# Measured durations in the planner of a two-block network kernel, and small-column 1/sqrt on ScalarE with a Newton step on VectorE instead of GpSimd's pow

## The chip, the cores and the metric

One core of one Trainium2 chip runs the whole program. The metric is the device time of one execution in microseconds. The five instruction streams of the core are called here PE (TensorE), ACT (ScalarE), DVE (VectorE), POOL (GpSimd) and SP (SyncE, which here only issues transfers).

## The reference

Two blocks run one after the other on one sequence of 512 rows of 1024 numbers in float32; each has two layers. Cut to the parts that the text speaks of:

```python
def _rmsnorm(x, g):
    y = xf * lax.rsqrt(jnp.mean(xf * xf, axis=-1, keepdims=True) + EPS)
    return (y * g.astype(jnp.float32)).astype(x.dtype)
...
for l in range(DEPTH):                      # first block, DEPTH = 2
    z = _rmsnorm(x, g_pre_mix[l]) @ w_in[l]
    y_f = _fourier_mix(zf, w_fourier[l])
    y_a = _window_attn(rope(zq), rope(zk), v, sink[l])
    mkv = _rmsnorm(mem, g_mem[l]) @ w_mem_kv[l]
    y_m = _memory_attn(zm, km, vm)
    y = concat([_rmsnorm(y_f), _rmsnorm(y_a), _rmsnorm(y_m)]) @ w_out[l]
    x = x + _rmsnorm(y, g_post_mix[l])
    h = _rmsnorm(x, g_pre_ffn[l])
    x = x + _rmsnorm((silu(gate) * up) @ w_ffn_out[l], g_post_ffn[l])
...
for l in range(DEPTH):                      # second block
    x = x + 0.5 * swiglu(rms_norm(x, ffn1_norm[l]), ffn1_w1[l], ffn1_w2[l])
    x = x + hybrid_mixer(rms_norm(x, mix_norm[l]), ...)   # RG-LRU, MLA attention, conformer convolution, gates
    x = x + 0.5 * swiglu(rms_norm(x, ffn2_norm[l]), ffn2_w1[l], ffn2_w2[l])
return rms_norm(x, final_norm)
```

## The kernel before

Activations lie transposed, as tiles of 128 features by 512 rows (slots named `s`, 100 of them); every product is made of three passes of TensorE over a high and a low half in a reduced type (h by l, l by h, h by h), so that one 128x128 block of a weight costs three matmuls of 512 columns. Weights come in three steps: POOL issues a transfer of the high half, ACT or DVE scales it by -1 into the low half's slot, and POOL issues a second transfer that adds the weight onto it. Sums build up in 8 PSUM banks (`ps`).

Nothing is issued in the order of the code. The code records every operation in a `Plan`; `price` (L391) gives each a length in us, and `schedule` (L423) is a list scheduler that plays the five engines against these lengths: an operation's due time comes from the running sum of TensorE's lengths ahead of its consumers, free slots and PSUM banks are counted, a transfer lands after a modelled time, and of the operations that are ready the one due first is taken. A `copy` or `scale` may go to ACT or DVE, whichever would be done first. The order that comes out is issued at L646, so all instructions of the trace stand on that one line, and groups have to be told apart by their tiles.

The root mean square of a norm is made in two ways. `inv` (L800) sums the squares with four or two one-column matmuls (`ps<-ones,s` with `128x1`), DVE makes `rms` (mean plus EPS, 128 partitions by 4 or 2 columns), POOL raises it to the power -1/2 in one instruction (`rinv<-rms,nhalf`), DVE multiplies an identity by it and a matmul (`ps<-s,ones`) spreads it over the partitions; there are 19 of these. `wide` (L819) makes the sum on all partitions with two matmuls (`ps<-s,onesr`) and then the root on ACT, the reciprocal and four more steps on DVE, all 512 columns wide. ACT's functions live in tables; a change from exp or silu to the root shows in the trace as `ACT_TABLE_LOAD`.

Of the kernel before, what the change touches and what calls it, by code (L numbers as in the profile page):

```python
# [15 lines left out]
AF = mybir.ActivationFunctionType  # L16
ALU = mybir.AluOpType
# [298 lines left out]
class Plan:  # L316
# [76 lines left out]
    def price(self, way, outs, ins):  # L393
        eng, fn, _, kw = way
        width = lambda v: int(np.prod(v.shape[1:]))
        n = width(outs[0]) if eng == "tensor" else max([width(v) for v in outs + ins if v.shape[0] > 1] or [1])
        psum = any(v.tile.psum for v in outs + ins)
        cols = sum(isinstance(kw.get(k), View) for k in ("scalar1", "scalar2", "scalar", "bias", "scale"))
        if eng == "sync":
            return 128 * n * 4 / 330e3  # L400
        if eng == "tensor":
            if fn == "transpose":
                return 0.11
            if ins[0].tile.dtype == F32:
                return 2 * max(0.107, 0.427 * n / 512)
            return max(0.107, 0.213 * n / 512 + 0.003)
        if eng == "scalar":
            return 0.093 + n * 0.833e-3 + 0.093 * (cols > 0) + (0.1 if "accum_out" in kw else 0.0)
        if eng == "vector":
            if fn == "reciprocal":  # L410
                return 0.07 + 6.25e-3 * n
            if fn in ("tensor_scalar", "tensor_copy", "memset") and not psum:
                return 0.07 + 0.52e-3 * n + 0.06 * (cols > 0)
            return 0.07 + 1.04e-3 * n + (0.06 if fn == "scalar_tensor_tensor" else 0.0)
        if fn == "dma_start":
            return 0.6
        if kw.get("op") == ALU.pow:
            return 0.95
        if fn == "tensor_scalar":
            return 0.25 + (3.36e-3 if cols else 0.65e-3) * n  # L420
        return 0.07 + 2.25e-3 * n

    def schedule(self):  # L423
# [28 lines left out]
        state = {"table": None, "dma": 0.0}  # L452
        now = 0.0
# [91 lines left out]
        while done < len(self.ops):  # L545
            moved = True
            while moved:
                moved = False
                for e in self.ENGINES:
                    while idle_at[e] <= now + 1e-9 and queues[e]:  # L550
                        op = choose(e, pe[front].need if front < len(pe) else 1e9)
# [17 lines left out]
                        if e == "sync":  # L569
                            state["dma"] = max(state["dma"], now + 0.5) + cost  # L570
                            op.end, idle_at[e] = state["dma"] + 1.6, now + 0.06
                        elif op.fn == "dma_start":
                            n = int(np.prod(op.kw["out"].shape[1:]))
                            passes = 2 if "accum_op" in op.kw else 1
                            state["dma"] = max(state["dma"], now + 1.0) + passes * 128 * n * 4 / 330e3
                            op.end = state["dma"] + 1.6
                        heapq.heappush(events, (op.end, op.index, op))
                        for t in op.tiles:
                            t.ends[e] = max(t.ends.get(e, 0.0), op.end)
# [26 lines left out]
            now = events[0][0]  # L606
            while events and events[0][0] <= now + 1e-9:
                op = heapq.heappop(events)[2]
# [54 lines left out]
class Net:  # L663
# [141 lines left out]
    def inv(self, parts, d, n=4):  # L805
        nc = self.nc
        pv = self.ps()
        for i, p in enumerate(parts):
            for j in range(n):
                nc.tensor.matmul(pv[:, j:j + 1], p[:, 128 * j:128 * j + 128], self.ones[:, 0:1],  # L810
                                 start=i == 0 and j == 0, stop=i == len(parts) - 1, skip_group_check=True)
        v = self.small(n, name="rms")
        nc.vector.tensor_scalar(out=v, in0=pv[:, 0:n], scalar1=1.0 / d, scalar2=EPS,
                                op0=ALU.mult, op1=ALU.add)
        r = self.small(n, name="rinv")
        nc.gpsimd.tensor_tensor(out=r, in0=v, in1=self.nhalf[:, 0:n], op=ALU.pow)
        return r

    def wide(self, parts, d):  # L819


        nc = self.nc
        ps = self.ps()
        for i, p in enumerate(parts):
            h, l = self.split_t(p)
            nc.tensor.matmul(ps, self.onesr, l, start=i == 0, stop=False)
            nc.tensor.matmul(ps, self.onesr, h, start=False, stop=i == len(parts) - 1)
        v = self.t()
        nc.vector.tensor_scalar(out=v, in0=ps, scalar1=1.0 / d, scalar2=EPS, op0=ALU.mult, op1=ALU.add)
        r = self.t()  # L830
        nc.scalar.activation(out=r, in_=v, func=AF.Sqrt)
        nc.vector.reciprocal(out=r, in_=r)
        self.tt(v, r, out=v)
        self.tt(v, r, out=v)
        nc.vector.tensor_scalar(out=v, in0=v, scalar1=-0.5, scalar2=1.5, op0=ALU.mult, op1=ALU.add)
        return self.tt(r, v, out=r)
# [912 lines left out]
```

## Time and profile before

| what | value |
|---|---|
| runs of the kernel before | 3479.14, 3483.54, 3483.74 us, median 3483.54 |
| the profiled execution's own time | 3481.36 us |
| its span (first to last instruction) | 3479.6 us |
| PE busy | 3404.2 us (98%), 16296 matmuls |
| DVE, ACT, POOL busy | 1923.0, 893.1, 1748.9 us |
| granted TensorE clock, mean of the span | 0.992 |

The span is one execution seen by the hardware profiler; busy time of an engine is the sum over its instructions. PE is the engine to look at, so what matters of the other engines is where PE waited for them. 1.9 us of the profiled execution's time lie outside the span.

### The profile page before, as it was taken

The page shows a single profiled execution, that of the slowest core. Times are in us where ns is not written, and L with a number is a line of the kernel's source. Part 1 is how long each engine was busy: PE and PEld are TensorE (multiplying, and loading weights), DVE is VectorE, ACT ScalarE, POOL GpSimd, SP SyncE. Part 2 cuts the span into 40 slices and gives each one's busy share as a digit, 9 for nine tenths or more (in the row PEclk, how much of TensorE's full clock was granted, in tenths as well). Part 3 has the DMA queues.
Part 4 walks back from the last instruction along what each step waited for, and adds up shares of the span by engine and source line. Part 5 has one row for each costly group of instructions (what it writes and reads, how often), then busy time and mean ns, then how long its engine had stood idle before and what let it go on. Part 6 is the DMA issues. An engine that isn't in the chain of part 4 may idle for free.

```text
span 3479.6 us, 44666 instructions
## 1 busy us (share of the span) xinstructions
PE 3404.2 (98%) x16296; PEld 2844.1 (82%) x16296; DVE 1923.0 (55%) x3916; ACT 893.1 (26%) x1732; POOL 1748.9 (50%) x2433
## 2 busy tenths in 40 slices
PE   6999999899999999999999999999999999999998
PEld 4788888778888988888888888888888888888887
DVE  7964433876432733259997534244423999744332
ACT  5741002543000301016723200010001573411000
POOL 2455464364446544653456544664465336654462
PEclk8999999999999999999999999999999999999999
DMA  6688897798789887985899977998799669998794
GB/s 174 145 186 184 164 207 148 156 193 183 153 169 208 207 181 157 239 212 103 172 197 249 220 152 158 220 204 200 150 225 219 130 130 222 230 239 160 158 202 104
DMA packets 360444, 635.93 MB, mean 183 GB/s; under 512 B 40608, under 2 KB 63904, under 8 KB 360224
## 3 DMA queue, kind: packets, MB, share of 16 engines
q0 software_dynamic: 346752, 612.56, 82.4%
q1 hardware_dynamic: 13472, 20.52, 1.9%
q8 instruction: 128, 2.10, 0.2%
q14 instruction: 92, 0.75, 0.1%
HBM read 624.00 MB, written 6.29 MB: 181 GB/s over the span
## 4 chain that ended last, share of the span: by engine, by line
PE 90%; DVE 4%; DMA 2%; issue 1%; ACT 1%; POOL 1%; SPq 0%; POOLq 0%; DVEq 0%; ACTq 0%
PE ps L646 90%; DVE s L646 4%; ACT s L646 1%; DMA s<-in_x 1%; POOL s L646 0%; DMA s<-in_b_in 0%; DMA s<-in_pos 0%; DMA s<-in_a_in 0%; DMA s<-s 0%; POOL rinv L646 0%; DVE mx L646 0%; DMA s<-in_a_out 0%; DMA s<-in_a_mk 0%; SPq L646 0%; DVE sp L646 0%
## 5 line engine op out<-in xcount | busy, mean ns | idle before, releaser
L646 PE MATMUL ps<-s 128*128 128x512 f32 (+2 forms) x15706 | 3350.9, 376 | 44.6 <-DVE s L646 32.4
L646 PEld LDWEIGHTS ps<-s 128*128 128x128 f32 (+1 forms) x15706 | 2775.6, 188 | 587.9 <-DVE s L646 29.7
L646 POOL DMA_DIRECT2D s<-in_b x1088 | 786.0, 1024 | 666.2 <-DVE s L646 312.2
L646 ACT ACTIVATE s<-s 128x512 fp32r<-128x512 f32 (+2 forms) x702 | 396.9, 601 | 1713.0 <-DVE s L646 1142.4
L646 DVE TENSOR_TENSOR s<-ps,s 128x512 f32<-128x512 f32 (+4 forms) x642 | 397.9, 637 | 580.8 <-PE ps L646 571.6
L646 DVE TENSOR_SCALAR s<-s 128x512 fp32r<-128x512 f32 (+2 forms) x847 | 341.5, 422 | 486.3 <-DMA s<-in_b 283.9
L646 POOL DMA_DIRECT2D s<-in_a_f x544 | 397.4, 1089 | 354.3 <-DVE s L646 199.3
L646 DVE TENSOR_TENSOR s<-s 128x512 f32<-128x512 f32 (+2 forms) x822 | 500.7, 626 | 64.1 <-ACT s L646 36.5
L646 POOL DMA_DIRECT2D s<-in_b_in x368 | 290.4, 1030 | 263.4 <-ACT s L646 84.0
L646 DVE SCALAR_TENSOR_TENSOR s<-s,vecs 128x256 fp32r<-128x256 f32 (+25 forms) x446 | 288.3, 680 | 6.3 <-ACT s L646 3.2
L646 ACT ACTIVATE s<-s,vecs 128x512 f32<-128x512 f32 (+2 forms) x221 | 139.5, 652 | 307.1 <-DVE s L646 294.2
L646 DVE SCALAR_TENSOR_TENSOR s<-ps,s 128x512 f32<-128x512 f32 (+1 forms) x33 | 22.3, 674 | 187.2 <-PE ps L646 187.0
L646 ACT ACT_TABLE_LOAD x68 | 87.2, 1283 | 42.0 <-DVE s L646 40.2
L646 ACT ACTIVATE s<-ps 128x512 f32<-128x512 f32 (+1 forms) x40 | 21.4, 534 | 274.0 <-PE ps L646 251.9
L646 DVE CAST s<-s 128x512 fp32r<-128x512 f32 x192 | 83.8, 436 | 6.5 <-DMA s<-in_pos 1.1
L646 POOL DMA_DIRECT2D s<-in_a_in x64 | 47.2, 931 | 76.2 <-DVE s L646 24.4
L646 DVE RECIPROCAL s<-s 128x128 f32<-128x128 f32 (+1 forms) x46 | 76.5, 1673 | 7.8 <-ACT s L646 7.8
L646 ACT ACTIVATE s<-s,nb 128x256 f32<-128x256 f32 (+3 forms) x128 | 70.6, 553 | 25.9 <-DVE nb L646 25.7
L646 POOL DMA_DIRECT2D s<-in_a_out x64 | 49.5, 1125 | 47.9 <-PE ps L646 30.1
L646 PE MATMUL ps<-ident,s 128*128 128x128 f32 x392 | 56.7, 275 | 14.2 <-DVE s L646 14.2
L646 ACT CAST s<-ps 128x256 fp32r<-128x256 f32 (+4 forms) x142 | 59.9, 455 | 34.0 <-PE ps L646 28.5
L646 POOL TENSOR_TENSOR rinv<-rms,nhalf 128x2 f32<-128x2 f32 (+1 forms) x19 | 20.8, 1165 | 92.4 <-DVE rms L646 91.2
(71 smaller groups left out, 869.6 us busy)
## 6 DMA issues: line engine op xcount, KB each, us to landing
s<-in_b POOLq DMA_DIRECT2D x1024, 256.0 KB, 6.4
s<-in_a_f POOLq DMA_DIRECT2D x512, 256.0 KB, 6.3
s<-in_b_in POOLq DMA_DIRECT2D x368, 256.0 KB, 6.2
s<-in_a_in POOLq DMA_DIRECT2D x64, 256.0 KB, 7.1
s<-in_a_out POOLq DMA_DIRECT2D x64, 256.0 KB, 6.3
s<-in_b_out POOLq DMA_DIRECT2D x64, 256.0 KB, 7.2
s<-in_b POOLq DMA_DIRECT2D x64, 128.0 KB, 6.5
s<-in_b_mo POOLq DMA_DIRECT2D x32, 256.0 KB, 6.0
```

What stands on the lines that cost most here:

```text
L646: getattr(getattr(nc, op.eng), op.fn)(*[real(v) for v in op.args], **{k: real(v) for k, v in op.kw.items()})
```

## The change

Every length in `price` is given a new number, and the planner's model of a transfer too: it now moves 240 to 250 GB/s in place of 330 and lands 4.0 us after its data in place of 1.6. A two-column or four-column root in `inv` is no longer POOL's one `pow` but six instructions: a root on ACT, then on DVE a reciprocal, two products, a scale-and-add and a product. Nothing else of the computation changes. The core of the diff:

```diff
         if eng == "sync":
-            return 128 * n * 4 / 330e3
+            return 128 * n * 4 / 240e3
...
-            return max(0.107, 0.213 * n / 512 + 0.003)
+            rows = ins[0].shape[0]
+            return max(0.059, 0.0135 + n / 2400.0) * (0.6 if rows == 64 else 1.0)
         if eng == "scalar":
-            return 0.093 + n * 0.833e-3 + 0.093 * (cols > 0) + (0.1 if "accum_out" in kw else 0.0)
+            return 0.2 + n * 0.82e-3 + 0.1 * (cols > 0) - 0.035 * psum + (0.19 if "accum_out" in kw else 0.0)
...
-            return 0.07 + 1.04e-3 * n + (0.06 if fn == "scalar_tensor_tensor" else 0.0)
+            return 0.15 + 1.05e-3 * n + 0.06 * (cols > 0) + (0.085 if "accum_out" in kw else 0.0)
         if fn == "dma_start":
-            return 0.6
+            return 0.75
...
-                            op.end = state["dma"] + 1.6
+                            state["dma"] = max(state["dma"], now + 1.0) + 128 * n * 4 / 250e3 * (1.3 if passes == 2 else 0.95)
+                            op.end = state["dma"] + 4.0
...
-        nc.gpsimd.tensor_tensor(out=r, in0=v, in1=self.nhalf[:, 0:n], op=ALU.pow)
+        self.rsqrt(r, v)
         return r
+
+    def rsqrt(self, r, v):
+
+        nc = self.nc
+        n = v.shape[-1]
+        t = self.small(4, name="rs")[:, 0:n]
+        nc.scalar.activation(out=r, in_=v, func=AF.Sqrt)
+        nc.vector.reciprocal(out=r, in_=r)
+        nc.vector.tensor_tensor(out=t, in0=v, in1=r, op=ALU.mult)
+        nc.vector.tensor_tensor(out=t, in0=t, in1=r, op=ALU.mult)
+        nc.vector.tensor_scalar(out=t, in0=t, scalar1=-0.5, scalar2=1.5, op0=ALU.mult, op1=ALU.add)
+        nc.vector.tensor_tensor(out=r, in0=r, in1=t, op=ALU.mult)
```

The new lengths move instructions on all engines. Counted over the whole program, the scales of low halves go from 595 on ACT and 970 on DVE to 706 and 859, the copies from 236 on ACT and 269 on DVE to 261 and 244, and the table loads from 68 to 71. Three places of PE's stream follow, before and now.

The first is the norm of the memory rows in the first layer. `ps<-ones,s` is its sum, `ps<-s,ones` spreads its 1/sqrt, the 128x128 products with `ident` are transposes of attention probabilities, the 64-row products apply probabilities, and the 128x256 products behind them are the memory's keys. Before:

```order
L646 MATMUL ps<-ones,s 128x1 x2
L646 MATMUL ps<-ident,s 128x128 x14
L646 MATMUL ps<-s,ones 128x256
L646 MATMUL ps<-ident,s 128x128 x6
L646 MATMUL ps<-s 64x256 x6
L646 MATMUL ps<-s 64x384 x6
L646 MATMUL ps<-s 128x256 x48
```

and now:

```order
L647 MATMUL ps<-ones,s 128x1 x2
L647 MATMUL ps<-ident,s 128x128 x10
L647 MATMUL ps<-s,ones 128x256
L647 MATMUL ps<-ident,s 128x128 x2
L647 MATMUL ps<-s 128x256 x36
L647 MATMUL ps<-ident,s 128x128 x8
L647 MATMUL ps<-s 64x256 x6
L647 MATMUL ps<-s 64x384 x6
L647 MATMUL ps<-s 128x256 x12
```

The spreading product stands 4 transposes earlier, and 36 of the 48 products of the keys now stand ahead of 8 transposes and the 12 products that apply probabilities.

The second is the entry of the MLA attention of the second block (first layer; the second layer reads alike). `ps<-s,onesr` is the broad sum of the second of its two norms, `ps<-s,ones` spreads the first norm's 1/sqrt, and the row that waits for `Activation` behind it is the first product of the values, whose input is the second norm's result. Before, from right behind the broad sum on:

```order
L646 MATMUL ps<-s 128x512 x2
L646 MATMUL ps<-s 128x512 [waits DMASW5_49]
L646 MATMUL ps<-s,ones 128x512 [waits DVE_49]
L646 MATMUL ps<-s 128x512 [waits DMASW0_49]
L646 MATMUL ps<-s 128x512 x10
L646 MATMUL ps<-s 128x512 [waits DMASW1_49]
L646 MATMUL ps<-s 128x512 x11
L646 MATMUL ps<-s 128x512 [waits DMASW2_49]
L646 MATMUL ps<-s 128x512 x10
L646 MATMUL ps<-s 128x512 [waits DMASW4_49]
L646 MATMUL ps<-s 128x512
L646 MATMUL ps<-s 128x512 [waits DMASW3_49,Activation_49]
```

and now:

```order
L647 MATMUL ps<-s,onesr 128x512 [waits DVE_49]
L647 MATMUL ps<-s,onesr 128x512
L647 MATMUL ps<-s 128x512 x5
L647 MATMUL ps<-s 128x512 [waits DMASW5_49]
L647 MATMUL ps<-s 128x512 x3
L647 MATMUL ps<-s,ones 128x512 [waits DVE_49]
L647 MATMUL ps<-s 128x512 x7
L647 MATMUL ps<-s 128x512 [waits DMAHW6_49]
L647 MATMUL ps<-s 128x512 [waits DMASW0_49,PE_49,Activation_49]
```

Between the broad sum and the first product of the values there stood 40 matmuls (3, the spreading one and 36); now there stand 18 (9, the spreading one, 7 and one float32 product of the keys' rotary part).

The third is the layer norm of the convolution branch (second block, first layer). The second row of the pair with `onesr` is its broad sum, the rows up to the last are products of other branches, and the last row, which waits for `DVE`, is the first product of the branch's output weight. Before:

```order
L646 MATMUL ps<-s,onesr 128x512
L646 MATMUL ps<-s 128x512 x4
L646 MATMUL ps<-s 128x512 [waits DMASW0_49]
L646 MATMUL ps<-s 128x512 [waits DMASW5_49]
L646 MATMUL ps<-s 128x512 x10
...
L646 MATMUL ps<-s 128x512 [waits DMASW3_49]
L646 MATMUL ps<-s 128x512 [waits DMASW1_49]
L646 MATMUL ps<-s 128x512 x7
L646 MATMUL ps<-s 128x512 [waits DVE_49]
```

and now:

```order
L647 MATMUL ps<-s,onesr 128x512
L647 MATMUL ps<-s 128x512
L647 MATMUL ps<-s 128x512 [waits DMASW0_49]
L647 MATMUL ps<-s 128x512 x10
...
L647 MATMUL ps<-s 128x512 [waits DMASW6_49]
L647 MATMUL ps<-s 128x512 [waits DMASW4_49]
L647 MATMUL ps<-s 128x512 x10
L647 MATMUL ps<-s 128x512 [waits DVE_49]
```

From the broad sum to the first product of the branch's output there stood 61 matmuls; now there stand 48, and the pair of the sum itself stands later among the products of the gates.

## Rows read from the trace of the kernel before

**Rows 1.** Page: busy time, share of span, instructions; the chain by engine.

```profile
PE 3404.2 (98%) x16296; PEld 2844.1 (82%) x16296; DVE 1923.0 (55%) x3916; ACT 893.1 (26%) x1732; POOL 1748.9 (50%) x2433
...
PE 90%; DVE 4%; DMA 2%; issue 1%; ACT 1%; POOL 1%; SPq 0%; POOLq 0%; DVEq 0%; ACTq 0%
```

**Rows 2.** Busy time by stretch (us, matmuls in brackets), then granted clock, DMA share, GB/s.

```profile
0.00:87.00 87.00, 54.14 (x268) 42.57 (x270) 68.75 (x155) 49.05 (x105) 20.48 (x33) 0.86 0.66 174
...
600.00:700.00 100.00, 82.84 (x571) 73.33 (x572) 86.98 (x244) 56.19 (x153) 36.16 (x51) 0.91 0.71 157
...
1000.00:1100.00 100.00, 100.00 (x443) 82.84 (x442) 32.46 (x66) 5.92 (x10) 62.07 (x88) 1.00 0.98 206
...
1600.00:1700.00 100.00, 98.67 (x490) 81.44 (x489) 95.70 (x208) 73.50 (x135) 35.41 (x48) 1.00 0.65 128
```

**Rows 3.** Who waited for whom: total us, times, longest.

```profile
PE ps L646 <- DVE s L646: 54.7, 20, 12.8
...
DVE s L646 <- POOL rinv L646: 11.4, 12, 2.7
```

**Rows 4.** Groups of instructions: busy us, mean ns, idle before, releaser.

```profile
L646 POOL TENSOR_TENSOR rinv<-rms,nhalf 128x2 f32<-128x2 f32 (+1 forms) x19 | 20.8, 1165 | 92.4 <-DVE rms L646 91.2 <-DVE sp L646 1.0
...
L646 ACT ACT_TABLE_LOAD x68 | 87.2, 1283 | 42.0 <-DVE s L646 40.2 <-PEq L1742 0.7
...
L646 DVE TENSOR_SCALAR s<-s 128x512 fp32r<-128x512 f32 (+2 forms) x847 | 341.5, 422 | 486.3 <-DMA s<-in_b 283.9 <-DMA s<-in_a_f 149.4 <-DMA s<-in_b_in 22.1
...
L646 DVE TENSOR_TENSOR sp<-sp,sp 128x4 f32<-128x4 f32 x20 | 3.0, 152 | 0.3
```

**Rows 5.** Timeline at the start: start, us, engine, instruction, idle before.

```profile
58.30 3.89 PE L646 MATMUL ps<-s 64*128 64x256 f32 x25 [7.39 <-DVE s L646]
```

**Rows 6.** Timeline at the memory norm of the first layer.

```profile
92.37 0.15 DVE L646 TENSOR_SCALAR rms<-ps 128x2 f32<-128x2 f32 x1
...
92.61 0.88 POOL L646 TENSOR_TENSOR rinv<-rms,nhalf 128x2 f32<-128x2 f32 x1 [2.16 <-DVE rms L646]
...
94.63 0.70 PE L646 MATMUL ps<-s,ones 128*128 128x256 f32 x2 [0.98 <-DVE s L646]
...
96.14 0.76 DVE L646 TENSOR_TENSOR s<-s 128x256 f32<-128x256 f32 x2
...
97.99 1.19 PE L646 MATMUL ps<-s 128*128 128x256 f32 x8 [0.28 <-PE ps L646]
```

**Rows 7.** PE's timeline at the boundary of the first block's layers.

```profile
621.19 0.63 PE L646 MATMUL ps<-s,onesr 128*128 128x512 f32 x2
...
644.87 3.36 PE L646 MATMUL ps<-s 64*128 64x256 f32 x21 [12.79 <-DVE s L646]
```

**Rows 8.** PE's timeline at the group norms, second layer.

```profile
751.66 2.08 PE L646 MATMUL ps<-s,ones 128*128 128x512 f32 x4 [0.83 <-DVE s L646]
```

**Rows 9.** Timeline at the MLA entry, first layer.

```profile
1553.79 0.63 PE L646 MATMUL ps<-s,onesr 128*128 128x512 f32 x2
...
1562.73 1.42 DVE L646 SCALAR_TENSOR_TENSOR s<-s,vecs 128x512 f32<-128x512 f32 x2
...
1563.52 0.72 ACT L646 ACTIVATE s<-s,vecs 128x512 fp32r<-128x512 f32 x1 [6.18 <-DVE s L646]
```

**Rows 10.** Timeline at the convolution branch's norm, first layer.

```profile
1850.00 0.72 PE L646 MATMUL ps<-s,onesr 128*128 128x512 f32 x2
...
1860.46 1.52 ACT L646 ACTIVATE s<-s,vecs 128x512 f32<-128x512 f32 x2 [1.22 <-DVE s L646]
...
1862.60 1.29 DVE L646 TENSOR_TENSOR s<-s 128x512 fp32r<-128x512 f32 x2
```

**Rows 11.** Timeline at the end of the program.

```profile
3469.81 0.70 POOL L646 TENSOR_TENSOR rinv<-rms,nhalf 128x2 f32<-128x2 f32 x1 [7.37 <-DVE rms L646]
...
3470.54 0.42 DVE L646 TENSOR_TENSOR s<-ident,rinv 128x256 f32<-128x256 f32 x1 [0.87 <-POOL rinv L646]
```

**Rows 12.** Page, transfers: KB of one, us from issue to landing.

```profile
s<-in_b POOLq DMA_DIRECT2D x1024, 256.0 KB, 6.4
```

More of the change, by code (lines that the diff above doesn't have):

```diff
@@ L399, in price @@
         if eng == "sync":
-            return 128 * n * 4 / 330e3
+            return 128 * n * 4 / 240e3
         if eng == "tensor":
             if fn == "transpose":
-                return 0.11
+                return 0.109
             if ins[0].tile.dtype == F32:
-                return 2 * max(0.107, 0.427 * n / 512)
-            return max(0.107, 0.213 * n / 512 + 0.003)
+                return 2 * max(0.056, 0.006 + n / 960.0)
+            rows = ins[0].shape[0]
+            return max(0.059, 0.0135 + n / 2400.0) * (0.6 if rows == 64 else 1.0)
         if eng == "scalar":
-            return 0.093 + n * 0.833e-3 + 0.093 * (cols > 0) + (0.1 if "accum_out" in kw else 0.0)
+            return 0.2 + n * 0.82e-3 + 0.1 * (cols > 0) - 0.035 * psum + (0.19 if "accum_out" in kw else 0.0)
         if eng == "vector":
             if fn == "reciprocal":
-                return 0.07 + 6.25e-3 * n
+                return 0.14 + 6.25e-3 * n
+            if fn == "tensor_tensor_scan":
+                return 1.22
             if fn in ("tensor_scalar", "tensor_copy", "memset") and not psum:
-                return 0.07 + 0.52e-3 * n + 0.06 * (cols > 0)
-            return 0.07 + 1.04e-3 * n + (0.06 if fn == "scalar_tensor_tensor" else 0.0)
+                return 0.16 + 0.525e-3 * n + 0.06 * (cols > 0)
+            return 0.15 + 1.05e-3 * n + 0.06 * (cols > 0) + (0.085 if "accum_out" in kw else 0.0)
         if fn == "dma_start":
-            return 0.6
+            return 0.75
         if kw.get("op") == ALU.pow:
-            return 0.95
-        if fn == "tensor_scalar":
-            return 0.25 + (3.36e-3 if cols else 0.65e-3) * n
+            return 0.75
         return 0.07 + 2.25e-3 * n
@@ L574, in schedule @@
                             passes = 2 if "accum_op" in op.kw else 1
-                            state["dma"] = max(state["dma"], now + 1.0) + passes * 128 * n * 4 / 330e3
-                            op.end = state["dma"] + 1.6
+                            state["dma"] = max(state["dma"], now + 1.0) + 128 * n * 4 / 250e3 * (1.3 if passes == 2 else 0.95)
+                            op.end = state["dma"] + 4.0
                         heapq.heappush(events, (op.end, op.index, op))
```

## The prediction

> **What bounds the kernel now.** I read the page first: PE is busy 3404.2 of 3479.6 us, and the chain that ended last lies on PE for 90% [rows 1]. So no other engine's total decides; what can change is PE's own work, which the change leaves as it is (16296 matmuls, the same three passes), or the 75.4 us that PE stands idle and what it loses beside. The table of stretches says where that is. In an undisturbed 100 us PE is busy throughout with 443 matmuls, which is 0.2257 us for one of 512 columns. It is short by 32.9 us in the first 87, by 17.2 from 600 to 700, and by only 1.3 from 1600 to 1700, although DVE is busy 95.70 there [rows 2]. Most of what PE waits for is DVE: 54.7 us in 20 waits, the longest 12.8 [rows 3]. These waits are dependency chains at the edges of layers, in which DVE and ACT work on something that PE needs at once. The question for a new order is therefore: at each such chain, how much later work of PE stands between its start and its first consumer? That I read from PE's order before and now; the durations come from rows alone.
>
> **The change, part by part.**
>
> The roots themselves. POOL loses 19 instructions of 1.165 us, which stand on DVE's way for 11.4 us in all [rows 3, 4]. In their place come an ACT root and five small steps on DVE. A product of four columns is 0.152 us, so DVE's five make 5 x 0.152 = 0.76 us, for 19 of them 14.4 us more on an engine that has 1923.0 [rows 1, 4]. The small ACT root isn't in the trace; it lies between nothing and POOL's 0.70 us, and I take 0.3. At the very end nothing hides it. There the root took POOL 0.70 us and DVE's product began at 3470.54, 0.73 after the root's start [rows 11]. Now 0.3 + 0.76 and the handovers make about 1.3, so +0.5 (0.3 to 1.1). The first of the two final norms has matmuls beside it and costs nothing; without them it would cost the same again. The new order has 3 table loads more, which at 1.283 us are 3.8 us of an ACT that is busy a quarter of the span [rows 1, 4]; where ACT stands idle ahead of the root the load goes into the idle time, so I add nothing (3.8 at most).
>
> The Trainium skill ("ScalarE: Activation LUTs", section "Table sets: the hidden batching unit") has exp and sqrt in different table sets, has each change pay a load of about 2.7 us, and advises to batch by set; that speaks against a root of ACT between exps. By its figure three loads would be an estimated 8 us at most; the trace's mean of 1.283 us [rows 4] decides, and the sum goes by that.
>
> The start. First scores come at 58.30 after an idle 7.39 that ends with DVE [rows 5]. DVE now makes seven adds of the memory's squares ahead of the rope products instead of later; by the row of two such adds, 0.38 us each [rows 6], that is 2.7 us. Two of its 512-wide steps that stood ahead of the first norm's end now stand behind it, 0.645 us each by the row of two [rows 10]; I take off 1.3: +1.4 (0 to 2.7).
>
> The memory norm of layer one (first pair of order listings). Before, `rms` stood at 92.37, the root took POOL 0.88, and the spreading product ran at 94.63 with a wait of 0.98, behind 14 transposes. The keys began at 97.99 with 0.28 of wait [rows 6]. Now DVE makes the five small steps between three mask steps of the next scores and one eviction, so the spreading factor is ready some 1.2 us later than before, at 95.8, and PE comes to it 4 transposes (0.5 us) sooner. Then only two transposes cover DVE's copy, adds, gain and split, about 2.4 us to the first operands of the keys: keys at about 98.9. So they begin 0.9 later, and 8 transposes and 12 products that were done by then (3.0 us) still have to run; the keys' 36 products themselves come at DVE's pace. That is +4; at best the later work covers all but 1, at worst nothing is regained and it is +7.
>
> The boundary of the first block's layers. From the broad sum at 621.19 to the first scores at 644.87 lie 23.7 us, at whose end PE waited 12.79 [rows 7]. In the new order the broad sum stands behind 143 products instead of 109: 34 narrow ones of 256 columns, about 0.12 us each, so 4.1 us later, and 47 instead of 82 cover what follows. DVE makes 81 instructions instead of 77 on that way. The chain starts later, but a part of that is a shorter wait ahead of it: +3 (0 to 5).
>
> The four pairs of group norms. POOL's roots queue behind its own transfers' issue; one place shows 0.83 of PE's wait [rows 8], and it is the last and longest of four such waits, 2.7 us together. A root on ACT doesn't queue there, but may need a load: -2 (-2.7 to +1.3, one load).
>
> The MLA entry, twice (second pair of listings). From the broad sum at 1553.79, DVE and ACT need until 1564.2 for the first operand of the values (STT from 1562.73, the gain on ACT from 1563.52 for 0.72) [rows 9]: 10.4 us. Before, 40 matmuls stood between, 9.0 us and the broad sum's own 0.6, so there was nearly no wait. Now there are 18, 4.1 us and 1 us for the float32 one; the chain gains about 0.9 because DVE no longer waits for POOL ahead of it. 10.4 - 0.9 - 0.6 - 5.1 leaves 3.8, and the sum starts some 0.5 later, since DVE now also makes the copy for it: about 4.4. While PE waits DVE gets ahead, so short waits behind the place shrink; that lies between nothing and all of it, and I give back a third, 1.4: +3 a layer, +6 (2 to 9).
>
> The convolution's norm, twice (third pair). The broad sum ran at 1850.00, the first silu on ACT at 1860.46, and DVE's split of it from 1862.60 [rows 10], so the operand is there at 1863.3, 13.3 us after. Before, 61 products took 0.5 + 13.8 = 14.3 us: no wait. Now 48 take 11.4: a wait of 1.9, and as the following operands come one per 1.7 us (two splits of 0.6 and a cast), 1.4 more by pace: +3.3 a layer, +6.6 (2 to 8).
>
> The rest of the scales and weights. 111 scales move from DVE to ACT. Both had idle time in the long stretches, where PE had no wait to lose: 0, with the low halves' lead times as the risk (rival three).
>
> Sum: 0.5 + 1.4 + 4 + 3 - 2 + 6 + 6.6 = **+19.5 us**, ends +2 and +33. On the profiled execution's 3481.36 that is 3500.9; the median of the runs, 3483.54, is 2.2 above that execution, and I put the time at 3502.
>
> **The rivals.**
>
> *The edges get faster.* The 111 scales taken off DVE, at a mean of 0.422 us, are 47 us [rows 4]. PE's waits for DVE total 54.7 [rows 3]; if 23 of these scales stood within the chains PE waits for, that would take away 9.7 us, and the new waits would have to stay out as well: 3481.4 - 9.7 = 3472. It decides from some 17 scales on (7 us). For it: edges are where DVE is the releaser. Against: in the boundary DVE has 81 instructions where it had 77, so it isn't relieved there.
>
> *The waits are only moved.* PE executes the same matmuls; where it waits at the entry of MLA, DVE, which is 95.70 busy [rows 2], gets ahead, and what follows runs without its own waits. Of the 19.5 then only the start, the end and half of the memory norm stay, about +4, and -2 of the group norms: 3483. For it: the waits in these places before were short and many. Against: from 1600 to 1700 PE was short by just 1.3 us, so there is little to regain.
>
> *The weights come late.* A transfer lands 6.4 us after its issue [rows 12], and the low half needs two with a scale between. In the MLA stretch the new order puts the second issues closer ahead of their use than before. A delay of DVE or ACT ahead of such an issue then reaches PE; ten waits of 2 us, a third of the flight, would add 20 on top of the sum: 3521. For it: ACT's share of the scales grows to 706 of 1565. Against: from 1600 to 1700 the stretch with the busiest DVE had nearly no wait [rows 2].
>
> *The table loads count.* The rule that mixed sets pay loads, fully on the path: 3 more loads at 1.283 are 3.8 us [rows 4] and, if the four roots between exps each held up PE by two, 8 x 1.283 = 10.3 more, on top of the sum: 3515. The rule named above (the Trainium skill, "ScalarE: Activation LUTs") is this one.
>
> **How the numbers follow.** Runs of before differ by 0.13%, so about 0.2%, 7 us, is what a measurement can tell from no change. Chances: my sum 0.57 (3490 to 3512); only moved 0.18 (3477 to 3490); faster edges 0.13 (3465 to 3476); late weights 0.07 and loads 0.05 (3512 to 3530). The range that leaves out about 2 in 10 is 3474 to 3518; the likeliest case's own is 3490 to 3512. Faster 0.14, within 0.2% 0.18, slower 0.68.
>
> **What would show it.** Right: in the new trace PE waits 3 to 5 us ahead of the first value product, some 2 us ahead of the convolution's output, over 2 us at the memory's spreading product and 12 to 17 before the second layer's scores; no `rinv` on POOL; 71 loads. The steps fall if those waits are under 1 us each, or if they are there and the stretch behind them is shorter by as much. The forecast is wrong as a whole if the long stretches change: if PE, at 443 matmuls per 100 us, was itself paced by something that the new order relieves, or if waits for transfers appear there.

## The result and the profile after

The changed kernel takes 3512.86 us (median of 4 runs, 3511.47 to 3514.76) where the kernel before, in the same session, takes 3483.64. The ratio is 1.0086, with a 95% interval from 1.007 to 1.0102: about 29 us slower. The forecast was slower too, at 3502 us; the measured time lies inside its range (3474 to 3518), but 0.9 us above the likeliest case's own (3490 to 3512). The span of the profiled execution is 3510.4 us, 30.8 more than before.

The page after, busy times and the chain by engine, answers to [rows 1]:

```profile
PE 3413.8 (97%) x16296; PEld 2853.9 (81%) x16296; DVE 1871.3 (53%) x3875; ACT 980.5 (28%) x1890; POOL 1726.3 (49%) x2414
...
PE 92%; DVE 5%; DMA 2%; ACT 1%; issue 0%; SPq 0%; POOL 0%; DVEq 0%; ACTq 0%; POOLq 0%
```

PE executes the same 16296 matmuls, but is busy 9.6 us longer, and stands idle 3510.4 - 3413.8 = 96.6 us instead of 75.4. DVE is busy 51.7 us less and ACT 87.4 us more. So the relief of DVE came, and PE didn't stand idle less for it. Who waits for whom, total us, times and longest (of before, [rows 3]):

```profile
PE ps L647 <- DVE s L647: 59.6, 27, 12.9
...
PE ps L647 <- ACT s L647: 25.4, 10, 6.7
```

PE's waits for DVE grew by 4.9 us. The waits for ACT, which were 5.1 us in 7 waits before, are now 25.4 in 10; 6.7 of that is the first wait of the program, which was 8.2 for DVE before. Busy time by stretch, as in [rows 2], after:

```profile
0.00:87.00 87.00, 53.99 (x256) 42.35 (x256) 70.04 (x160) 43.13 (x95) 20.93 (x34) 0.84 0.66 176
...
600.00:700.00 100.00, 77.93 (x515) 68.39 (x514) 78.97 (x222) 51.12 (x134) 32.65 (x46) 0.88 0.61 137
...
700.00:800.00 100.00, 92.77 (x552) 78.39 (x552) 68.02 (x170) 59.21 (x144) 56.49 (x82) 0.95 0.90 191
...
1000.00:1100.00 100.00, 100.00 (x443) 82.87 (x442) 29.97 (x60) 9.53 (x16) 57.61 (x80) 1.00 0.94 199
...
1500.00:1600.00 100.00, 96.37 (x414) 78.00 (x413) 59.91 (x118) 27.96 (x49) 48.22 (x69) 0.97 0.80 182
...
1600.00:1700.00 100.00, 98.89 (x496) 81.87 (x494) 81.98 (x198) 68.67 (x135) 28.75 (x38) 1.00 0.50 96
...
2700.00:2800.00 100.00, 95.95 (x441) 77.36 (x440) 71.76 (x168) 48.96 (x98) 41.88 (x57) 0.98 0.74 157
```

and three of these stretches before, which [rows 2] doesn't have:

```profile
700.00:800.00 100.00, 96.00 (x584) 82.17 (x583) 70.72 (x165) 49.04 (x119) 59.87 (x85) 0.98 0.87 190
...
1500.00:1600.00 100.00, 99.49 (x454) 80.73 (x453) 73.52 (x161) 39.18 (x75) 52.09 (x73) 1.00 0.83 186
...
2700.00:2800.00 100.00, 99.52 (x481) 81.06 (x480) 94.56 (x220) 62.41 (x118) 34.20 (x45) 1.00 0.60 121
```

The undisturbed 1000 to 1100 is as it was, 443 matmuls. What is lost is lost at the edges: PE is busy 77.93 from 600 to 700 (82.84 before), and 96.37 and 95.95 in the two stretches with an MLA entry (99.49 and 99.52 before). The column before the last two is the granted clock: 0.88 against 0.91 from 600 to 700, 0.95 against 0.98 from 700 to 800, and 0.97 and 0.98 against 1.00 at the MLA entries. In such stretches the 9.6 us of more busy time lie: behind some waits the same matmuls run slower for a while. Ten microseconds behind the first MLA entry's wait, and six around a wait in layer two's attention, read:

```profile
1580.00:1590.00 10.00, 10.00 (x39) 8.09 (x38) 8.02 (x15) 4.46 (x10) 1.22 (x2) 0.83 0.35 54
714.00:720.00 6.00, 4.21 (x11) 3.24 (x12) 4.00 (x12) 6.00 (x22) 4.41 (x8) 0.51 0.55 89
```

I also worked out from all starts of matmuls, for each stretch, how much longer PE took than at the spacing that its shapes have undisturbed (0.227 us at 512 columns, 0.120 at 256, and so on). That counts waits and the slower clock together, but not the wait ahead of the program's first matmul, which fell from 8.20 us to 6.72:

| stretch of the span before (us) | before | after | difference | forecast |
|---|---|---|---|---|
| start, 0 to 60 | 28.1 | 29.5 | +1.4 | +1.4 |
| memory norm and around, 60 to 160 | 13.8 | 17.9 | +4.1 | +4 |
| boundary of the first block's layers | 21.2 | 25.5 | +4.3 | +3 |
| group norms of layer one | 1.5 | -0.4 | -1.9 | \} -2 |
| layer two's attention and group norms | 8.0 | 14.5 | +6.5 | \} |
| up to the second block's mixer | -0.6 | 0.7 | +1.3 | 0 |
| MLA entry and attention, two layers | 14.2 | 23.7 | +9.5 | +6 |
| convolution's norm, two layers | 0.1 | 4.9 | +4.8 | +6.6 |
| end | 2.5 | 3.8 | +1.3 | +0.5 |
| all, with the small rest | 87.0 | 119.0 | +32.0 | +19.5 |

Now the places. At the memory norm, against [rows 6]; start, us, engine, instruction, idle before:

```profile
93.03 0.16 DVE L647 TENSOR_SCALAR rms<-ps 128x2 f32<-128x2 f32 x1 [1.90 <-PE ps L647]
...
93.23 0.20 ACT L647 ACTIVATE rinv<-rms 128x2 f32<-128x2 f32 x1 [1.03 <-DVE rms L647]
...
94.53 0.16 DVE L647 RECIPROCAL rinv<-rinv 128x2 f32<-128x2 f32 x1
...
96.08 0.17 DVE L647 COPY mem_r<-rinv 128x2 f32<-128x2 f32 x1
...
96.76 1.22 PE L647 MATMUL ps<-s,ones 128*128 128x256 f32 x2 [2.61 <-DVE s L647]
...
100.21 1.65 PE L647 MATMUL ps<-s 128*128 128x256 f32 x6 [1.81 <-DVE s L647]
```

The root on ACT itself takes 0.20 us, less than POOL's 0.88. But DVE's reciprocal starts only at 94.53, because two masks of the next scores and an eviction stand ahead of it on DVE, and its later steps stand between more of them; the copy of the result starts 3.05 us after `rms`. The spreading product waits 2.61, the keys 1.81 more. The table load for this root starts at 90.92 and is over before `rms` is there, so it isn't on the path.

At the MLA entry, first layer, against [rows 9]; PE's rows, and ACT's gain that they wait for:

```profile
1568.26 0.74 PE L647 MATMUL ps<-s,onesr 128*128 128x512 f32 x2 [0.20 <-DVE s L647]
...
1571.39 3.24 PE L647 MATMUL ps<-s 128*128 128x512 f32 x9
...
1578.02 12.36 PE L647 MATMUL ps<-s 128*128 128x512 f32 x42 [3.39 <-ACT s L647]
...
1577.24 0.72 ACT L647 ACTIVATE s<-s,vecs 128x512 fp32r<-128x512 f32 x1 [4.14 <-DVE s L647]
```

After nine fillers, the spreading product, seven more fillers and the float32 product PE waits 3.39 us for ACT, whose gain ends at 1577.96, 9.7 us after the broad sum. The second layer reads alike. At the convolution's norm, against [rows 10]:

```profile
1896.47 0.73 PE L647 MATMUL ps<-s,onesr 128*128 128x512 f32 x2 [1.31 <-DVE s L647]
...
1897.04 11.07 PE L647 MATMUL ps<-s 128*128 128x512 f32 x48
...
1909.58 15.71 PE L647 MATMUL ps<-s 128*128 128x512 f32 x68 [1.47 <-DVE s L647]
```

48 products, 11.07 us of them, and a wait of 1.47, where 1.9 was forecast; a wait of 1.31 ahead of the broad sum comes on top. At the boundary of the first block's layers, against [rows 7]:

```profile
628.66 0.63 PE L647 MATMUL ps<-s,onesr 128*128 128x512 f32 x2
...
629.13 5.78 PE L647 MATMUL ps<-s 128*128 128x256 f32 x47
...
638.69 1.12 PE L647 MATMUL ps<-ident,s 128*128 128x128 f32 x4 [3.78 <-DVE s L647]
...
651.42 8.83 PE L647 MATMUL ps<-s 64*128 64x256 f32 x46 [11.62 <-DVE s L647]
```

The broad sum is later and 47 products follow instead of 82; the wait is split in two, 3.78 and 11.62, which is 2.6 more than the 12.79 before. In layer two's attention there is a wait that the forecast didn't have at all:

```profile
715.79 4.21 PE L647 MATMUL ps<-s 128*128 128x512 f32 x9 [4.80 <-ACT s L647]
```

PE waits 4.80 us for ACT, and its next 9 matmuls take 4.21 us, 0.47 each, about twice the undisturbed 0.2257: the lower of the two clock levels, as the granted 0.51 of that stretch says (above). At the end of the program, against [rows 11]:

```profile
3499.89 0.20 ACT L647 ACTIVATE rinv<-rms 128x2 f32<-128x2 f32 x1 [0.89 <-DVE rms L647]
...
3501.12 0.42 DVE L647 TENSOR_TENSOR s<-ident,rinv 128x256 f32<-128x256 f32 x1
```

From the root's start to DVE's product are 1.23 us, where it was 0.73: the 0.5 of the forecast. The groups of the new root over the whole program, as in [rows 4]:

```profile
L647 ACT ACT_TABLE_LOAD x71 | 91.1, 1283 | 38.6 <-DVE s L647 31.7 <-DVE nb L647 2.8 <-issue 2.3
...
L647 ACT ACTIVATE rinv<-rms 128x2 f32<-128x2 f32 (+1 forms) x19 | 3.9, 204 | 15.1 <-DVE rms L647 15.0
...
L647 DVE RECIPROCAL rinv<-rinv 128x2 f32<-128x2 f32 (+1 forms) x19 | 3.1, 165 | 3.4 <-ACT rinv L647 3.4
...
L647 DVE TENSOR_SCALAR rs<-rs 128x2 f32<-128x2 f32 (+1 forms) x19 | 3.4, 179 | 0.4
```

### The profile page after: what moved, and what is told of

Same layout as the page of the kernel before. It is cut to its first block, busy times and chain, and to the rows that moved or that the text cites. A ratio compares the mean times of both kernels' runs of the same rounds, so it can differ in the third digit from the quotient of the medians.

```text
span 3510.4 us, 44913 instructions
## 1 busy us (share of the span) xinstructions
PE 3413.8 (97%) x16296; PEld 2853.9 (81%) x16296; DVE 1871.3 (53%) x3875; ACT 980.5 (28%) x1890; POOL 1726.3 (49%) x2414
## 4 chain that ended last, share of the span: by engine, by line
PE 92%; DVE 5%; DMA 2%; ACT 1%; issue 0%; SPq 0%; POOL 0%; DVEq 0%; ACTq 0%; POOLq 0%
PE ps L647 92%; DVE s L647 4%; ACT s L647 1%; DMA s<-in_b_in 1%; DMA s<-in_x 0%; DMA s<-in_b_uq 0%; DMA s<-in_pos 0%; DVE mx L647 0%; DMA s<-s 0%; ACT L647 0%; SPq L647 0%; POOL s L647 0%; DVE nb L647 0%; DVE rc L647 0%; DVE rs L647 0%
## 5 line engine op out<-in xcount | busy, mean ns | idle before, releaser
L647 PE MATMUL ps<-s 128*128 128x512 f32 (+3 forms) x15706 | 3363.7, 377 | 58.6 <-DVE s L647 31.8
L647 ACT ACTIVATE s<-s 128x512 fp32r<-128x512 f32 (+3 forms) x812 | 460.5, 603 | 1458.8 <-DVE s L647 1048.6
L647 DVE TENSOR_TENSOR s<-ps,s 128x512 f32<-128x512 f32 (+5 forms) x642 | 397.7, 637 | 800.6 <-PE ps L647 791.9
L647 DVE TENSOR_SCALAR s<-s 128x512 fp32r<-128x512 f32 (+1 forms) x737 | 295.2, 421 | 237.7 <-DMA s<-in_b 119.5
L647 DVE SCALAR_TENSOR_TENSOR s<-s,vecs 128x256 fp32r<-128x256 f32 (+26 forms) x446 | 286.0, 680 | 8.5 <-ACT s L647 5.2
L647 ACT CAST s<-s 128x512 fp32r<-128x512 f32 x74 | 45.7, 619 | 139.4 <-DVE s L647 125.1
L647 DVE CAST s<-s 128x512 fp32r<-128x512 f32 (+1 forms) x168 | 72.6, 432 | 6.5 <-DMA s<-in_pos 1.1
L647 PEld LDWEIGHTS ps<-ident,s 128*128 128x128 f32 x392 | 48.7, 143 | 31.3 <-DVE s L647 20.1
```

The lines of the kernel that those rows point to most:

```text
L647: getattr(getattr(nc, op.eng), op.fn)(*[real(v) for v in op.args], **{k: real(v) for k, v in op.kw.items()})
```

## The experiments

Ratios are to the kernel before, run beside each version; medians of different versions come from different sessions, in which the kernel before lay between 3481.70 and 3483.79 us. The theory to be tested was the forecast's: the loss comes from the order that the new lengths make, place by place. The rivals: the longer root makes it; the transfer model makes it; or the order of before is a lucky one and nearly any other would lose as much.

**The root alone, in the old order.** The plan is made with pow and the old lengths; where the order has pow, six instructions are issued.

```diff
         for op in self.schedule():
+            if op.kw.get("op") == ALU.pow:
+                r, v = real(op.kw["out"]), real(op.kw["in0"])
+                t = pools["sm"].tile([128, 4], F32, name="rs", tag="rs", bufs=4)[:, 0:v.shape[-1]]
+                nc.scalar.activation(out=r, in_=v, func=AF.Sqrt)
+                nc.vector.reciprocal(out=r, in_=r)
...
+                continue
```

> Planner and prices of before, so the order of before; only where the old order issues POOL's pow do the six instructions of the new root stand. If the loss comes from the moved order: +0.5 at the end of the program and at most 1 us at each of three or four places where PE waits for a root, so +0 to +5 us on before. If the longer root is what costs: +20 to +30 us.

3495.40 us, ratio 1.0033 (1.0021 to 1.0045). This version also exchanged two powers of another formula (a softplus), which changes that part of the computation, so it was run again with the 19 roots of norms alone (`and op.kw["out"].tile.tag == "rinv"`).

> As root_in_place, but only the 19 roots of norms are exchanged; the two power instructions of another formula stay on GpSimd. If the loss of 13 us seen there is the longer root on chains that PE waits for, it comes out again but for the part at the MLA entries: +9 to +14 us on before, with the waits at the memory norm's spreading product (3.4 us), at a group norm (2.2 us) and before a spreading product in the second layer (2.5 us). If it came from the wrongly exchanged power: within 4 us of before.

3493.68 us, ratio 1.0036 (1.0023 to 1.0049): about 12 us. So the wrongly exchanged power had no part that can be told from noise, and the root does cost something when nothing is planned for it: of the first version's two expectations both missed, +0 to +5 and +20 to +30. PE's rows at two spreading products, in the first and in the second layer of the first block:

```profile
167.84 1.21 PE L656 MATMUL ps<-s,ones 128*128 128x512 f32 x2 [1.92 <-DVE s L656]
...
740.21 1.10 PE L656 MATMUL ps<-s,ones 128*128 128x512 f32 x2 [2.21 <-DVE s L656]
```

In the old order DVE's five steps stand in one block at pow's place. The second of these waits was 0.57 before. But the steps aren't all: at both places, and at the memory norm, where PE waits 3.43 (0.98 before), a table load stands directly ahead of the root, and the plan, made with pow, knows nothing of it. At the memory norm:

```profile
93.83 0.15 DVE L656 TENSOR_SCALAR rms<-ps 128x2 f32<-128x2 f32 x1
...
94.45 1.28 ACT L649 ACT_TABLE_LOAD   x1
95.74 0.20 ACT L649 ACTIVATE rinv<-rms 128x2 f32<-128x2 f32 x1
...
95.98 0.17 DVE L650 RECIPROCAL rinv<-rinv 128x2 f32<-128x2 f32 x1 [1.61 <-ACT rinv L649]
```

The load is 1.28 of the 2.45 us by which the spreading product comes later behind `rms` than it did with pow. At the roots that need no load PE waits at most 0.66 in this version, but for the very last one of the program. The table above, for this kernel, has its loss at the memory norm (16.4 for 13.8) and the first layer's group norms (5.3 for 1.5).

**The new lengths with pow.**

```diff
-        self.rsqrt(r, v)
+        nc.gpsimd.tensor_tensor(out=r, in0=v, in1=self.nhalf[:, 0:n], op=ALU.pow)
```

> All new prices, but POOL's pow as before. 48 products instead of 61 still stand ahead of the first layer's convolution output, and the memory's spreading product stands behind 7 transposes. If the prices' order is the cause: +18 to +30 us on before. If the longer root is the cause: within 5 us of before.

3508.41 us, ratio 1.0067 (1.0051 to 1.0083): about 23 us, 26 by the medians. The lengths make most of the loss without the new root, as the theory has it. With the planner knowing it, the root adds some 3 to 4.5 us (3512.86 - 3508.41, medians of two sessions whose kernels before differ by 1.1), which is no more than the intervals leave open. The places are the same ones: with pow PE waits 1.25 at the memory norm's spreading product and 2.50 at its keys, and 3.78 and 3.77 at the MLA entries.

**The changed kernel with the old transfer model.**

```diff
-            return 128 * n * 4 / 240e3
+            return 128 * n * 4 / 330e3
...
-            return 0.75
+            return 0.6
...
-                            state["dma"] = max(state["dma"], now + 1.0) + 128 * n * 4 / 250e3 * (1.3 if passes == 2 else 0.95)
-                            op.end = state["dma"] + 4.0
+                            state["dma"] = max(state["dma"], now + 1.0) + passes * 128 * n * 4 / 330e3
+                            op.end = state["dma"] + 1.6
```

> The changed kernel with the old model of transfers (330 GB/s, 1.6 us to land, issue 0.6); the new lengths of the engines and the new root stay. The MLA entries have 39 fillers again instead of 18, the memory norm keeps its 10 transposes. If each place costs what PE's order there says: the two waits of 3.75 us at the MLA entries go, so about 8 us below the changed kernel, +22 on before. If the new transfer model is the whole cause: within 5 us of before. If it has no part: as the changed kernel, +29.

3505.50 us, ratio 1.006 (1.0042 to 1.0079): 6 to 7 us below the changed kernel, where about 8 was expected. Its MLA entry:

```profile
1579.60 0.62 PE L647 MATMUL ps<-s,onesr 128*128 128x512 f32 x2
...
1582.32 17.79 PE L647 MATMUL ps<-s 128*128 128x512 f32 x72
...
1601.64 2.11 PE L647 MATMUL ps<-s 128*128 128x512 f32 x8 [1.53 <-DVE s L647]
```

72 products follow without a break; 1.53 us of wait come behind them. The loss at the two entries is 12.7 us where the changed kernel has 23.7, but at the start and at the layer boundary it is higher (32.3 for 29.5, 28.5 for 25.5).

**The new transfer model alone**, on the kernel before (the same lines the other way).

> The kernel before with the new model of transfers alone; lengths of the engines and pow as before. MLA entries have 38 fillers (40 before), the convolution 61, the memory norm is ordered as before. If PE's order at these places decides: within 5 us of before. If the transfer model is the cause: +20 or more.

3487.08 us, ratio 1.0012 (1.0002 to 1.0021). Within 5 us, as expected: that model isn't the cause by itself.

**The values held back at the MLA entry.** The changed order, with two groups of value products and their consumers put behind the 18 products that followed.

```diff
+    HELD = ((7588, 7603, 15), (12742, 12757, 15))
+    def held(self, order):
+        pe = [op for op in order if op.eng == "tensor"]
+        for lo, hi, n in self.HELD:
+            groups = {pe[i].kw["out"].tile if not pe[i].args else pe[i].args[0].tile for i in (lo, lo + 1)}
+            late = {op for op in pe[lo:hi] if groups & set(op.tiles)}
+            end = order.index(pe[hi + n - 1]) + 1
+            for op in order[:end]:
+                if op not in late and late & op.preds:
+                    late.add(op)
+            order = [op for op in order[:end] if op not in late] + [op for op in order[:end] if op in late] + order[end:]
```

> The changed kernel's order, but at the two MLA entries the first two groups of value products, and what needs them, stand behind the 18 products that followed them, so that 36 instead of 18 lie between the broad sum and the first value product. If the two waits of 3.75 us come from that place in PE's order: they go, 5 to 8 us below the changed kernel. If the chain behind the norm is late for another reason and PE is only made to wait elsewhere: within 2 us of the changed kernel.

3509.48 us, ratio 1.0081 (1.0066 to 1.0096), where the changed kernel has 1.0086. The medians differ by 3.4 us, but the kernel before was 1.9 us faster as well where the two were run side by side (3481.70 for 3483.64), and the spans of the two profiled executions differ by 1.2. So the second expectation, within 2 us, is the nearer one. The wait of 3.39 us is gone, and a new one stands further on:

```profile
1569.35 0.73 PE L661 MATMUL ps<-s,onesr 128*128 128x512 f32 x2 [0.21 <-DVE s L661]
...
1572.43 11.72 PE L661 MATMUL ps<-s 128*128 128x512 f32 x45
...
1586.58 5.74 PE L661 MATMUL ps<-s 128*128 128x512 f32 x17 [2.44 <-DVE s L661]
```

So the first product did come too early; but behind it DVE is late too, and most of the wait is moved, not saved (2.44 of 3.39). The loss in the two stretches falls from 23.7 to 21.6 us only, against 14.2 before.

**The new lengths of ScalarE and VectorE alone**, and **those of TensorE alone**, each on the kernel before (the lines of `price` of those engines, as in the change).

> The kernel before with the new lengths of ScalarE and VectorE alone; PE's lengths, transfers and pow as before. The order puts 47 fillers at the MLA entries (40 before, 18 in the changed kernel) and 48 at the convolution's norm (61 before). If PE's order at the places decides: the convolution waits as in the changed kernel (3 and 1.7 us), the MLA entries don't, in all +5 to +15 us on before. If these lengths are the whole cause: +20 or more.

3507.17 us, ratio 1.0076 (1.0061 to 1.0091): 25 us, more than the places I had counted. The MLA entries are clean, as expected. At the boundary of the first block's layers PE waits 5.22 and 11.40 us, where it waited 12.79 before. The convolution's wait stands ahead of its broad sum, and a new one at the memory attention:

```profile
114.16 2.08 PE L648 MATMUL ps<-s 128*128 128x256 f32 x8 [4.84 <-DVE mx L648]
...
1894.39 0.73 PE L648 MATMUL ps<-s,onesr 128*128 128x512 f32 x2 [2.17 <-DVE s L648]
```

These two engines' new lengths are those of one instruction by itself, and that isn't what the planner does with them: it lets an engine begin its next instruction when the length is over. In the trace instructions in a row overlap. Rows of DVE in the changed kernel:

```profile
1560.95 2.48 DVE L647 TENSOR_TENSOR s<-ps,s 128x512 f32<-128x512 f32 x4
...
1563.35 0.68 DVE L647 TENSOR_TENSOR s<-s 128x512 f32<-128x512 f32 x1
```

One takes 0.68 us, four in a row take 2.48, so they start 0.60 apart; the old price is 0.602, the new one 0.688. ACT's scales of 512 columns take 0.617 and start 0.521 apart (medians of 164 that follow one another); the old price is 0.520, the new one 0.620. So for work in a row the old lengths are the nearer ones on these two engines. No run has the spacing as their length beside the other new numbers, so what this is worth stays open.

> The kernel before with the new lengths of TensorE alone. 30 fillers at the MLA entries, 60 and 58 at the convolution's norm, the memory norm nearly as before. If the places decide: some 1 to 2 us at each MLA entry, in all 0 to +8 us on before. If TensorE's lengths are the whole cause, as they set every due time: +20 or more.

3513.76 us, ratio 1.0094 (1.0077 to 1.0111): 32 us, as much as the whole change, where 0 to 8 was expected. The waits, in the first layer's group norms and at the convolution of both layers of the second block:

```profile
192.74 3.13 PE L647 MATMUL ps<-s,ones 128*128 128x512 f32 x4 [3.38 <-DVE s L647]
...
1878.44 3.98 PE L647 MATMUL ps<-s 128*128 128x512 f32 x10 [3.56 <-DVE s L647]
...
3031.82 1.22 PE L647 MATMUL ps<-s,onesr 128*128 128x512 f32 x2 [5.02 <-DVE s L647]
```

Three new waits of 3 to 5 us again, one at the group norms, where the changed kernel had none, and two at the convolution, where they are longer than in the changed kernel. The value products at the MLA entries wait 1.55 each, as expected. TensorE's new lengths are nearer to the trace than the old ones (0.2268 for 512 columns, where the spacing is 0.227 and the old price 0.216). The split of the scales is as before (704 `ACTIVATE s<-s` on ACT in the page, 702 before, 812 in the changed kernel), so a loss of this size doesn't need the scales to move between the engines. The parts don't add: 32 and 25 alone, 29 with everything together.

**Small shifts.** One engine's lengths 2% longer, nothing else:

```diff
-        op.cost = {w[0]: self.price(w, outs, ins) for w in ways}
+        op.cost = {w[0]: self.price(w, outs, ins) * (1.02 if w[0] == "vector" else 1.0) for w in ways}
```

> The kernel before with all lengths of VectorE in the planner 2% longer, nothing else; 42 fillers at the MLA entries, 62 at the convolution, the memory norm as before. If the size of the wrong places decides (big changes of lengths move consumers close behind their chains): within 5 us of before. If the order of before is a lucky one, and nearly any other order loses as much: +15 us or more.

3481.42 us, ratio 0.9993 (0.9983 to 1.0002).

> The kernel before with all lengths of TensorE in the planner 2% longer, which shifts every due time; 40 fillers at the MLA entries, 60 at the convolution. If big changes are needed to lose: within 5 us of before. If nearly any other order loses: +15 us or more; the new lengths of TensorE alone lost 32.

3486.75 us, ratio 1.0013 (1.0003 to 1.0022).

> The kernel before with all lengths of ScalarE 2% longer; the places of PE's order stand as in before. If big changes are needed to lose: within 3 us of before. If nearly any other order loses: +10 us or more.

3487.73 us, ratio 1.0014 (1.0004 to 1.0023), 4 to 5 us in place of the 3 that the theory allowed.

> The changed kernel with all lengths of VectorE 2% longer; 20 instead of 18 fillers at the MLA entries, the convolution and the memory norm as in the changed kernel. If the measured lengths lead to these places as such: +26 to +32 us on before, as the changed kernel. If the changed kernel's order is only an unlucky one: 10 us or more below it.

3507.32 us, ratio 1.0065 (1.005 to 1.008): 5.5 us below the changed kernel, between what the two sides had; it is still 23 above the kernel before. Four small shifts, on either kernel, move the time by no more than some 5 us, and don't bring one kernel near the other. An order of before that any small change would lose doesn't survive three of them. They test orders near the old one; whether most orders far from it lose 25 us or more isn't shown. That old lengths are better because they had been fitted to this program is not shown; no run here shows how they came about.

No version beat the kernel before. The nearest, with VectorE's lengths 2% up, is the same within its interval.

## Why the prediction was right

The direction and the mechanism held: a moved order, and waits at the edges of layers. Most places held too. The size was 29 us for the 19.5 of the sum, and several terms met their number by chance.

- *What bounds it.* The long stretches stayed at 443 matmuls per 100 us; nothing but the edges moved. Right.
- *Start.* +1.4 forecast, +1.4 in the table, but the table leaves out the first wait, which fell by 1.5. With it the start lost next to nothing, and the first scores come at 58.94 instead of 58.30. The wait ahead of them did grow, from 7.39 to 10.52, and waits before it shrank by about as much. That the numbers agree is luck.
- *Memory norm.* +4 forecast, +4.1 measured. The spreading product came 3.73 us after `rms` and the keys 7.18 after it, for 3.4 and 6.5 in the forecast (95.8 and 98.9, with `rms` at 92.37). The agreement to 0.1 is in part luck: from 60 to 160 PE's waits grew by only 1.1 us together, and the granted clock was 0.50 from 95.3 to 105.5 (1.00 before), which the forecast had at nothing. With pow kept the stretch loses as much to about 0.1 us, so it is the order that costs here and not the longer root.
- *Boundary.* +3 forecast, +4.3 measured; 11.62 of wait ahead of the first scores and 3.78 further ahead, 15.4 together, inside the 12 to 17 named as a sign.
- *MLA entries.* The wait at the first value product was forecast as 4.4 and was 3.39 in idle time (3.75 beyond the undisturbed spacing), but the stretches lost 9.5 us instead of 6. The step that was mis-sized is what follows the wait. The forecast gave back 1.4 a layer; by the spacing of matmuls some 1.2 came back in the first layer and 0.5 in the second. And it had nothing for the clock: behind the waits 512-column matmuls start 0.43 apart instead of 0.227, until 1583.5 and 2744.0, the lower level of 1.2 GHz, which costs some 2.6 and 1.6 us. Holding the products back showed that DVE behind the entry is late as well, so that a wait taken away here comes back further on.
- *Convolution.* +6.6 forecast, 4.8 measured. The wait at the first product was 1.47 for 1.9; the pace term behind it, 1.4, didn't show, a wait of 1.31 ahead of the broad sum came unforeseen, and the second layer had only one of the two waits (1.39).
- *The group norms*, -2: in the first layer the table has -1.9, but not for the reason given. With the new lengths and pow still on POOL, PE has no wait over 0.5 us there either, so the order took the wait away and not the emptier queue of POOL. In the second layer this step failed: the stretch lost 6.5 us, most of it in a wait of 4.80 for ACT that I had not looked for in the order, with no table load ahead of it. I looked at the root there and not at the attention ahead of it.
- *The roots themselves*, +0.5: the end shows this very 0.5 in its last half, 1.3 with the first half's delay. Over the program the root costs some 3 to 4.5 us in its own plan (pow kept) and 12 put into the old order. The sum had counted these inside the places for the memory norm and MLA, and only in part.
- *Table loads.* 71, as read from the order, three more than before. In the order with 65 loads (ScalarE's and VectorE's lengths alone) the time was 25 us up, so their number didn't set it. The rival by the Trainium skill's rule ("ScalarE: Activation LUTs", "Table sets: the hidden batching unit") isn't borne out in the changed kernel, where no load stands on the way of the waits at the memory norm, at the layer boundary, in layer two's attention and at the MLA entry. With the root put into the old order it is, at three places, with up to 1.28 us each; the loads take 1.283 us in the mean.
- *The clock.* The sum priced waits only. PE is busy 9.6 us longer with the same matmuls, at a lower granted clock behind waits; that is a third of the 30.8, and part of each place's difference in the table.
- *The ends.* The lower ends of the terms add up to 2.6 and the upper ones to 34.1, where the forecast has +2 and +33; nothing hangs on it.

The other rivals: the edges didn't get faster, though DVE did get 51.7 us of relief. Moved waits were seen most clearly in the experiment with the values held back; in the changed kernel little of what was lost came back. Late weights: PE waited 2.8 us in all for transfers, less than before (4.3).

What stays open: why the new lengths of TensorE alone, whose sum over the program sets every due time, cost 32 us, when the same lengths with all others cost 29. The runs show the waits (3.38, 3.56, 5.02) and not which of the new numbers makes each of them. That a place's loss follows from the count of matmuls alone isn't shown either: at the MLA entries it went away where the plan itself put 39 fillers back (12.7 us, 14.2 before), and hardly moved where 36 were put there by hand (21.6).

## What to carry to other kernels

A list scheduler's lengths are its parameters, and lengths taken from a trace are not by themselves a better order: here those of TensorE and those of ScalarE and VectorE cost 32 and 25 us alone and 29 together with the rest, while 2% shifts moved the time by no more than some 5. Ask first what the planner does with a length: where it stands for the time until the engine's next instruction, the spacing in a row is the number to compare, and not the length of one. Judge such a change by counting, for each chain through the elementwise engines, the matmuls between its start and its first consumer in the old and in the new order, and price the difference with rows; that named most of the places where PE then waited. It gave the memory norm and the layer boundary to within 1.3 us, the first of them partly by chance, as slower matmuls behind the waits have to be counted too. Look through all places, and not only at those that the edit names: the one that was left out was the largest miss. And a function moved to ACT brings its table load: if the plan doesn't know of it, it can stand right on the chain.

## What was not expected of the hardware

After a wait of 4.80 us PE's next nine 512-column matmuls took 0.47 us each instead of 0.2257, the lower clock level; such a wait costs more than its length. Not each wait does: around the convolution's waits of 1.31 and 1.47 the granted clock is 1.00 (1800 to 1900 and 1900 to 2000 us). A root of 2 or 4 columns on ACT takes 0.204 us, in the lower half of the range I had taken from POOL's 0.70. A table load can run ahead of the wait of the root that needs it: in the changed kernel's memory norm it was over at 92.20, and the root waited for `rms` until 93.23.
